# Two whole gate-and-up blocks of each FFN replaced by a tenth seven-product pair

## The chip, the cores and the metric

The kernel runs on one core of a Trainium2 chip. The metric is the device time of one execution in microseconds (us). The engines are TensorE (PE, with its weight load PEld), VectorE (DVE), ScalarE (ACT), GpSimd (POOL) and SyncE (SP, which issues most DMAs). Each engine works off its own list of instructions in order.

## The reference

A trunk of two layers over 512 tokens of width 1024, in float32. Layer 0 has multi-head latent attention, layer 1 chunked attention with a relative bias; each is followed by a SwiGLU feed-forward network (FFN) of width 2816. The change is in the FFN and in the step into it:

```python
x = x + rms_norm(y, attn_post_g[layer])
h = rms_norm(x, ffn_pre_g[layer])
f = swiglu(h, ffn_w_gate[layer], ffn_w_up[layer], ffn_w_down[layer])
x = x + rms_norm(f, ffn_post_g[layer])

def swiglu(h, w_gate, w_up, w_down):
    return (jax.nn.silu(h @ w_gate) * (h @ w_up)) @ w_down
```

## The kernel before

Every float32 operand is split into a high and a low part (`split`: ACT casts `hi`, DVE subtracts to get `lo`, lines 144 and 145), and every product is three matmuls, hi x hi, lo x hi and hi x lo. Tensors are held transposed: 128 features on the partitions, 512 tokens along the row, so x is eight tiles of 128x512.

`ffn` (line 1134), called once per layer, does this:

- `out_proj` makes the attention's output projection in two halves of tokens, h = 0 and 1. `Post` adds up the squares of the result on PE (`tot`), takes the root on POOL, spreads it over the partitions on PE (`bc`), and adds the normed result to x, which `fetch` reads from memory ahead of the projection.
- The FFN's width is 22 blocks of 128. The first two blocks' gate and up (four PSUM banks, `b`) are made by `half(0)` and `half(1)`, 256 tokens each, as soon as that half of x is there. The pre-norm's row factor `rb` is applied only afterwards, to the gate.
- Blocks three and four follow as whole products of 512 columns (`proj`). While PE does these, `blocks_of` prepares four combined inputs `tb` (tiles `th`, `tl`, out of the scaled copies `xg` and the differences `t`), and the norm's `tot` and `bc` are done in between. `gt` is then the gated tile.
- The other 18 blocks are nine pairs in `products` (line 1517): a two-by-two scheme by seven products (j = 0 to 6) instead of eight, of 24 matmuls with 256 columns each, accumulated in the banks `be` (products 0 and 6), `al` (1, 3, 4, 5) and `ga` (2). Copies to `gt` and `ut` on ACT and sums on DVE put the results together.
- `down` then makes the last product of the FFN, also by seven products.

The weights come through `Feed`, a planned list: `load` issues the DMA into a ring of five tiles `raw`, `split` makes `whi` and `wlo` two steps ahead of the product. A `Pair` also needs sums of its four weight quarters: two of them are made by DMAs that POOL issues and that add into a tile already loaded (`begin`; `issue_after` holds them behind the last power on POOL), two by DVE (`sums`). For the first pair all of them are made by DVE. `behind(ins)` writes an instruction behind another on its engine.

The order on each engine is set by the scheduler out of the program order and these constraints.

Of the kernel before, what the change touches and what calls it, by code (L numbers as in the profile page):

```python
# [10 lines left out]
F32 = mybir.dt.float32  # L11
# [8 lines left out]
KT = D // P  # L20
# [7 lines left out]
N_WHOLE = 4  # L28
# [40 lines left out]
def trunk(ctx: ExitStack, tc: tile.TileContext, a, out):  # L69
# [80 lines left out]

    class Pair:
# [4 lines left out]
        def __init__(self, src):  # L156
            self.src, self.raw, self.then, self.made = src, {}, None, False

        def tile(self, n, pool_=wp, tag="raw", bufs=5):
            t = pool_.tile([P, 1024], F32, tag=tag, name=name_("raw"), bufs=bufs)  # L160
            nc.sync.dma_start(t, self.src[n])
            return t

        def begin(self):

            r, self.made = self.raw, True
            r[0] = r[3] = r[6] = self.tile(2, wide[0], "sum", 2)
            r[4] = self.tile(2, wide[0], "sum2", 2)
            for j, n in ((0, 3), (4, 0)):
                with tc.issue_after(last_pow[0].ins):  # L170
                    nc.gpsimd.dma_start(r[j], self.src[n], accum_op=OP.add)  # L171

        def load(self, j):

            if j == 0:
                if not self.made:
                    self.raw[4] = self.tile(2, wide[0], "sum2", 2)
                self.raw[5] = self.tile(3)
            elif j in (1, 2):
                self.raw[j] = self.tile(j - 1)  # L180

        def sums(self, j):
            def plus(t, x, y):
                V.tensor_tensor(t, x, y, op=OP.add)

            r = self.raw
            if j == 0 and not self.made:
                r[0] = r[3] = r[6] = wide[0].tile([P, 1024], F32, tag="sum", name=name_("raw"), bufs=2)
                plus(r[0], r[4], r[5])
            elif j in (3, 6):  # L190
                plus(r[j], r[j], r[j // 3])
            elif j == 4 and not self.made:
                plus(r[4], r[4], r[1])
            elif j == 1 and self.then:
                self.then.begin()
# [68 lines left out]
    class Feed:  # L264


        def __init__(self):
            self.plan, self.raw, self.ready, self.pos, self.room = [], [], [], 0, {}
            self.behind, self.gate, self.low = {}, None, None
# [4 lines left out]
        def add_pairs(self, src):  # L274

            n = src.shape[0]
            pairs = [Pair(src[p]) for p in range(n)]
            for p, pair in enumerate(pairs):
                pair.then = pairs[p + 1] if p + 1 < n else None
                for j in range(7):  # L280
                    self.plan.append((pair, 1024, j, None))
# [7 lines left out]
        def load(self, i):  # L289
            while len(self.raw) <= min(i, len(self.plan) - 1):  # L290
                src, n, j, _ = self.plan[len(self.raw)]
                if isinstance(src, Down):
                    src.load(*j)
                    self.raw.append(None)
                    continue
                if isinstance(src, Pair):
                    src.load(j)
# [314 lines left out]
    class Post:  # L612
# [54 lines left out]
        def apply(self, x, h, each, to=None):  # L667
            c = HALF[h]
            for k in range(KT):
                t = self.y[k][:, c]  # L670
                with first(80 * h):
                    V.tensor_tensor(t, t, self.r[h][:, c], op=OP.mult)
                    if to is None:
                        V.tensor_tensor(x[k][:, c], x[k][:, c], t, op=self.op)
                    else:
                        (nc.gpsimd if k in (0, 2, 4) else V).tensor_tensor(to(k), x[k][:, c], t, op=self.op)
                    each(k, h)

    def fetch(src, make=U):
        x = []  # L680
        for k in range(KT):
            t = make(name="x")
            nc.sync.dma_start(t, src[:, k])
            x.append(t)
        return x

    def out_proj(rhs, n_k, post, have, n_last, late):
# [35 lines left out]
        for h in range(2):  # L723
# [17 lines left out]
            if not h:  # L741
                feed.ahead(2 if late else 3)
# [40 lines left out]
    def plan_ffn(i):  # L783
        for c in range(4):
            feed.add(a["w_gu0"][i, c], 1024, room="h")
        for f in range(N_WHOLE - 2):
            for c in range(2):
                feed.add(a["w_gu"][i, f, c], 1024)
        feed.add_pairs(a["w_pair"][i])
        feed.add_down(a["w_down"][i])  # L790
# [343 lines left out]
    def ffn(i, x_src, osp, firsts, late=()):  # L1134
# [10 lines left out]
        x = fetch(x_src)  # L1145
        post = Post(G_APOST[i], H)
        last = out_proj(osp, KT, post, firsts, 2, late)
# [25 lines left out]
        tb = []  # L1173
        more = blocks_of(x, G_FPRE[i], H, tb)
        next(more)
        b = [bank(), bank()]
        rest = proj(2, KT, 4, xs, b)
        some(rest, 3)
        v = sx.sum.total()
        r = rstd(v)  # L1180
        eps = sp.tile([P, 4], F32, tag="eps", name=f"eps_{i}", bufs=1)
        V.tensor_scalar(eps, v, EPS, None, op0=OP.mult)
        some(rest, 7)
        rb = spread_sb(r)
        next(more)
        banks.extend(b)
        hid = Hidden(H)


        for f in range(N_WHOLE):  # L1190
            if f < 3:
                b = banks[2 * f:2 * f + 2]
                if f == 2:
                    run(rest)
            else:
                b = [bank(), bank()]
                run(proj(2, KT, 4, xs, b))
            t = U(name="gt")
            V.tensor_tensor(t, b[0], rb, op=OP.mult)
            nc.scalar.activation(t, t, AF.Silu)  # L1200
            h = hid.room()
            V.scalar_tensor_tensor(h, t, -1.0, b[1], op0=OP.mult, op1=OP.mult)
            hid.add(h)
            if f == 1:
                next(more)
        products(xs, tb, rb, hid, by_tokens(H) if i else None)
# [108 lines left out]
    def blocks_of(x, gain, make, out):  # L1315
# [3 lines left out]
        for k in range(KT // 2):  # L1319
            out.append([(U(F32R, "th"), U(F32R, "tl")) for _ in range(2)])  # L1320
# [9 lines left out]
        for k in K2:  # L1330
# [3 lines left out]
            split(*cut(out[k][0], A1), m[:, A1])  # L1334
        yield
        for k in K2:
# [3 lines left out]
            split(*out[k][1], n)  # L1340
        yield

    class After:
# [3 lines left out]
        def __init__(self, layer, eps, make):  # L1347
# [4 lines left out]
            self.x, self.later = None, []  # L1352
# [74 lines left out]
        def during(self, j, i):  # L1427
            if j == Down.E3 and i == 1:
                self.x = fetch(a["mid"])
                self.split = Split(self.x, None)  # L1430
# [89 lines left out]
    def products(xs, tb, rb, hid, aside=None):  # L1520
# [5 lines left out]
                  [cut(xs[k + K2], A1) for k in range(K2)]]  # L1526
        pairs = (NF - N_WHOLE) // 2
        for p in range(pairs):
            al, ga = [], []
            be = [bank("t" if p % 2 else "s", "be") for _ in range(2)]  # L1530
            gate = [U(name="gt") for _ in range(2)]
            up_ = [U(name="ut") for _ in range(2)]
            for j in range(7):
                if aside is not None and p and j in (0, 1, 3, 5):
                    next(aside, None)
# [8 lines left out]
                for e in range(2):  # L1544
# [10 lines left out]
                    elif j == 1:  # L1555
                        nc.scalar.copy(t[:, A0], o)
                    elif j == 2:
                        V.tensor_tensor(t[:, A0], t[:, A0], o, op=OP.add)
# [6 lines left out]
                    else:  # L1565
                        V.tensor_tensor(t[:, A1], t[:, A1], o, op=OP.add)
                        V.tensor_tensor(t, t, rb, op=OP.mult)
                        nc.scalar.activation(t, t, AF.Silu)
                        h = hid.room()
                        V.tensor_tensor(h, t, u, op=OP.mult)  # L1570
                        hid.add(h)
# [212 lines left out]
def _layout(i):  # L1784
# [37 lines left out]
    o["w_gu"] = np.stack([np.stack([_chunks(gu[l], fc(f), 4) for f in range(2, N_WHOLE)]) for l in range(2)])  # L1822
# [35 lines left out]
```

## Time and profile before

| what | value |
|---|---|
| median of three runs | 1105.42 us (1103.71 to 1106.43) |
| the profiled execution | 1105.07 us |
| its span in the profile | 1103.3 us |
| mean granted clock of TensorE | 0.997 |
| HBM traffic | 145 GB/s over the span |

A row of the trace gives the start in us, the duration (of all instructions, where "x4" says that several are put together), the engine, the source line, the operation with output<-input, and in brackets how long the engine stood idle before it and for whom. A row of the chain of waits gives the start, the duration, the engine and the number of instructions put together.

### The profile page before, as it was taken

How to read it: one execution, taken by the hardware profiler on the slowest of the kernel's cores; microseconds unless marked ns; L12 is line 12 of the kernel's file. 1: busy time of each engine (PE TensorE's matmuls, PEld its weight loads, DVE VectorE, ACT ScalarE, POOL GpSimd, SP SyncE). 2: the span in 40 equal slices, each digit the busy share in tenths (PEclk: the TensorE clock that was granted, in tenths of full speed). 3: DMA queues.
4: the chain of work that ended last, by engine and by line, in shares of the span. 5: the costliest groups of instructions: out<-in, count | busy, mean ns of one | idle time of the engine just before them, and what ended most of it. 6: DMA issues, size and time to landing. Idle time of an engine off the chain costs nothing.

```text
span 1103.3 us, 19079 instructions
## 1 busy us (share of the span) xinstructions
PE 1092.4 (99%) x6893; PEld 978.8 (89%) x6893; DVE 908.5 (82%) x1659; ACT 678.3 (61%) x1323; POOL 117.1 (11%) x181
## 2 busy tenths in 40 slices
PE   9999999999999999999999999999999999999997
PEld 6887889999999998888888888889899999998885
DVE  7787747988878889978858898758988889789977
ACT  7575737655555556668636767657645555556675
POOL 2211100101000001500000110000100010001401
PEclk9999999999999999999999999999999999999999
DMA  7344226447787757961555677634638888758913
GB/s 240 120 116 142 62 68 238 143 116 184 171 202 184 180 167 248 164 191 49 190 153 156 173 192 186 168 121 161 198 103 214 228 207 223 216 178 249 171 29 76
DMA packets 88334, 181.47 MB, mean 164 GB/s; under 512 B 26816, under 2 KB 28608, under 8 KB 88240
## 3 DMA queue, kind: packets, MB, share of 16 engines
q1 hardware_dynamic: 74752, 147.10, 43.1%
q0 software_dynamic: 13056, 32.73, 16.4%
q8 instruction: 54, 0.88, 0.3%
q10 hardware_dynamic: 432, 0.44, 0.1%
q14 instruction: 40, 0.33, 0.1%
HBM read 148.88 MB, written 10.88 MB: 145 GB/s over the span
## 4 chain that ended last, share of the span: by engine, by line
PE 97%; DVE 1%; ACT 1%; issue 1%; DMA 0%; POOL 0%; DVEq 0%; POOLq 0%; SPq 0%; ACTq 0%
PE al L1550 19%; PE b L377 11%; PE b L378 11%; PE b L379 11%; PE be L1550 9%; PE al L1306 8%; PE be L1306 5%; PE ga L1550 5%; PE de L1306 3%; PE ga L1306 3%; PE pt L561 2%; PE b L1707 2%; PE b L1107 1%; PE sc L1699 1%; PE sc L1698 1%
## 5 line engine op out<-in xcount | busy, mean ns | idle before, releaser
L144 ACT CAST whi<-raw 128x1024 fp32r<-128x1024 f32 (+3 forms) x220 | 221.0, 1006 | 205.6 <-PE al L1550 71.5
L145 DVE TENSOR_TENSOR wlo<-raw,whi 128x1024 fp32r<-128x1024 f32 (+3 forms) x220 | 255.8, 1164 | 67.1 <-ACT whi L144 66.1
L1550 PE MATMUL al<-th,whi 128*128 128x256 f32 x432 | 122.8, 284 | 0.0
L1550 PE MATMUL al<-th,wlo 128*128 128x256 f32 x432 | 121.0, 280 | 0.0
L1550 PE MATMUL al<-tl,whi 128*128 128x256 f32 x432 | 121.0, 280 | 0.0
L377 PE MATMUL b<-xh,whi 128*128 128x512 f32 x234 | 96.7, 415 | 0.0
L378 PE MATMUL b<-xl,whi 128*128 128x512 f32 x234 | 91.8, 392 | 0.0
L379 PE MATMUL b<-xh,wlo 128*128 128x512 f32 x234 | 91.7, 392 | 0.0
L1550 PEld LDWEIGHTS al<-th,whi 128*128 128x128 f32 x432 | 81.3, 188 | 2.2
L1550 PEld LDWEIGHTS al<-th,wlo 128*128 128x128 f32 x432 | 81.3, 188 | 0.2 <-DVE wlo L145 0.2
L1550 PEld LDWEIGHTS al<-tl,whi 128*128 128x128 f32 x432 | 81.3, 188 | 0.0
L548 ACT ACTIVATE p<-p,mn 128x128 f32<-128x128 f32 (+1 forms) x96 | 54.1, 563 | 36.0 <-DVE mn L546 34.1
L145 DVE TENSOR_TENSOR ptl<-pt,pth 128x128 fp32r<-128x128 f32 (+1 forms) x96 | 46.6, 485 | 30.5 <-ACT pth L144 29.6
L145 DVE TENSOR_TENSOR wlo<-wd,whi 128x512 fp32r<-128x512 f32 x86 | 56.3, 684 | 14.6 <-ACT whi L144 14.4
L144 ACT CAST whi<-wd 128x512 fp32r<-128x512 f32 x86 | 49.8, 618 | 25.0 <-PE al L1306 10.7
L144 ACT CAST pth<-pt 128x128 fp32r<-128x128 f32 (+1 forms) x96 | 40.3, 422 | 32.2 <-PE pt L561 31.3
L171 POOL DMA_DIRECT2D raw<-in_w_pair x32 | 28.1, 895 | 285.9 <-DVE ut L1562 84.1
L379 PEld LDWEIGHTS b<-xh,wlo 128*128 128x128 f32 x234 | 43.9, 188 | 9.9 <-DVE wlo L145 0.3
L1306 PE MATMUL al<-whi,pl 128*128 128x512 f32 x132 | 51.5, 390 | 0.0
L1306 PE MATMUL al<-wlo,ph 128*128 128x512 f32 x132 | 51.4, 389 | 0.0
L1306 PE MATMUL al<-whi,ph 128*128 128x512 f32 x132 | 51.4, 389 | 0.0
L377 PEld LDWEIGHTS b<-xh,whi 128*128 128x128 f32 x234 | 44.2, 189 | 5.7 <-ACT whi L144 0.2
(320 smaller groups left out, 3391.2 us busy)
## 6 DMA issues: line engine op xcount, KB each, us to landing
raw<-in_w_pair SPq DMA_DIRECT2D x88, 512.0 KB, 4.6
raw<-in_w_pair POOLq DMA_DIRECT2D x32, 512.0 KB, 7.6
wd<-in_w_down SPq DMA_DIRECT2D x54, 256.0 KB, 6.0
raw<-in_w_o SPq DMA_DIRECT2D x16, 512.0 KB, 4.0
raw<-in_w_gu SPq DMA_DIRECT2D x16, 512.0 KB, 4.7
raw<-in_w_down SPq DMA_DIRECT2D x16, 512.0 KB, 4.3
raw<-in_w_qkb SPq DMA_DIRECT2D x16, 512.0 KB, 3.5
wd<-in_w_down POOLq DMA_DIRECT2D x22, 256.0 KB, 5.0
```

The source lines that it names most:

```text
L144: return (nc.scalar.copy(dst_hi, src), V.tensor_tensor(dst_lo, src, dst_hi.bitcast(F32), op=OP.subtract))
L145: V.tensor_tensor(dst_lo, src, dst_hi.bitcast(F32), op=OP.subtract))
L171: nc.gpsimd.dma_start(r[j], self.src[n], accum_op=OP.add)
L377: nc.tensor.matmul(o, l[0], r[0], start=start, stop=False)
L378: nc.tensor.matmul(o, l[0], r[1], start=False, stop=False)
L379: last_mm[0] = nc.tensor.matmul(o, l[1], r[0], start=False, stop=stop)
L548: nc.scalar.activation(p[:, :n], p[:, :n], AF.Exp, bias=mn[:, :1], scale=-1.0, accum_out=self.sums[:, qt:qt + 1])
L561: nc.tensor.transpose(t[:, kt * P:(kt + 1) * P], p[:, kt * P:(kt + 1) * P], ident)
L1107: nc.tensor.matmul(o[:, q_], va[kt][:, part, v_], pt[:, kt, q_], start=n + kt == 0, stop=n == 2 and kt == NQT - 1)
L1306: nc.tensor.matmul(to[e], l[c], r[d], start=j < 4 and k == 0 and n == 0, stop=k == NF // 2 - 1 and n == 2, skip_group_check=True)
L1550: nc.tensor.matmul(o, l[c], r[d], start=first_ and n == 0, stop=k == K2 - 1 and n == 2, skip_group_check=True)
L1707: nc.tensor.matmul(o[:, q_], vv, pt[:, kt, q_], start=pt is pth and kt == 0, stop=pt is ptl and kt == NQT - 1)
```

## The change

- `N_WHOLE` falls from 4 to 2: blocks three and four become a tenth pair, which runs first, directly behind `half(1)`. The weights `w_gu` are gone.
- The first pair takes its products in the order 1, 2, 0, 3, 6, 4, 5 (`FIRST_TURN`). Its weight sums are all made by accumulating DMAs of POOL's queue: `begin` is called in the h = 0 step of `Post`, and `chain` adds one sum into the next, from SBUF to SBUF.
- `fetch` of x moves into `out_proj`, between its two halves, behind the weights' loads.
- The banks of the first two blocks are copied to SBUF by ACT (`kept`, tiles `fu`), and their gates are done later. The weight of product 3 is split into a room of its own ("u", tiles `wu`).
- The two steps of `blocks_of` and the weight splits are tied to one another by `feed.behind`. The squares of x are summed in the second pair (p = 1). The root is called at its product 6 and `bc` at product 0 of the third pair (p = 2); in the order both `tot` and `bc` come to stand in that product.
- Gates are put in a list `units` and taken from it one by one at j = 1, 3 and 5 of the pairs p = 2 to 6, and at once in p = 7 to 9; in layer 1 the transposes of x (`aside`) are spread over the pairs from p = 4.

```diff
-N_WHOLE = 4
+N_WHOLE = 2
...
+    FIRST_TURN = (1, 2, 0, 3, 6, 4, 5)
...
+        def chain(self):
+
+            self.add(3, self.raw[0])
+            self.add(6, self.raw[3])
...
+            if not h:
+                with behind(feed.loaded):
+                    next(p for p, *_ in feed.plan[feed.pos:] if isinstance(p, Pair)).begin()
...
-                feed.ahead(2 if late else 3)
+                feed.ahead(2 if late else 4)
+                feed.loaded = get_x(feed.loads[feed.pos + (4 if late else 5)])
...
-        sx.squares(0)
-        post.apply(x, 1, sx.each)
+        base = feed.pos
+        pair = feed.plan[base][0]
+        pair.chain()
+        feed.behind[base + 2] = feed.behind[base + 3] = post.apply(x, 1, sx.each)
+        tb, hid = [], Hidden(H)
+        more = blocks_of(x, G_FPRE[i], H, tb)
+        next(more)
+        feed.ahead(3)
         run(half(1))
-        sx.squares(1)
...
+        kept = [H(name="fu") for _ in banks]
+        for t, b in zip(kept[:2], banks[:2]):
+            nc.scalar.copy(t, b)
+        turned = list(next(more))
+        feed.behind[base + 4] = turned
+        with behind(turned[0]):
+            for t, b in zip(kept[2:], banks[2:]):
+                empty = nc.scalar.copy(t, b)
...
+        def step():
+            feed.split(base + 4)
+            with behind(feed.low):
+                turned[:] = next(more)
+            feed.behind[base + 5] = turned
+
+        side = {(0, 2): step, (1, 1): lambda: sx.squares(0), (1, 4): lambda: sx.squares(1), (1, 6): norm, (2, 0): spread_}
+        units = [lambda f=f: gate(*kept[2 * f:2 * f + 2]) for f in range(N_WHOLE)]
...
+            make = U if p > 6 or p == 5 else hid.make
...
+            for j in (range(7) if p else FIRST_TURN):
+                if (p, j) in side:
+                    side[p, j]()
+                if p > 1 and j in (1, 3, 5) and units:
+                    units.pop(0)()
```

PE, layer 0, from the last matmuls ahead of the step in question. Before, the first pair's first product (`be`) follows the end of block four (`b`):

```order
L377 MATMUL b_2790<-xh_2293,whi_2791 128x512
L378 MATMUL b_2790<-xl_2294,whi_2791 128x512
L379 MATMUL b_2790<-xh_2293,wlo_2792 128x512
L1550 MATMUL be_2858<-th_2606,whi_2821 128x256 [waits Activation_49]
L1550 MATMUL be_2858<-tl_2607,whi_2821 128x256
L1550 MATMUL be_2858<-th_2606,wlo_2822 128x256 [waits DVE_49]
```

After, `half(1)` is followed at once by products 1, 2, 0 and 3 of the first pair; this is the end of product 3, the first matmul of product 4 (whi_2776) and the start of product 6 (whi_2700):

```order
L1584 MATMUL al_2671<-tl_2476,wu_2529 128x256
L1584 MATMUL al_2671<-th_2475,wu_2530 128x256
L1584 MATMUL al_2670<-th_2465,whi_2776 128x256 [waits Activation_49]
L1584 MATMUL be_2664<-xh_2291,whi_2700 128x256 [waits Activation_49]
L1584 MATMUL be_2664<-xl_2292,whi_2700 128x256
L1584 MATMUL be_2664<-xh_2291,wlo_2701 128x256 [waits DVE_49]
```

One matmul of product 4 now stands ahead of product 6, and both wait for ACT. ACT, layer 0, where the combined inputs' last casts (`th`, 512 wide) are made. Before, they stand among the weight casts of the first pair, during the whole blocks:

```order
L144 CAST whi_2821<-raw_2819 128x1024 [waits PE_49,Activation_49]
L144 CAST th_2608<-t_590_2625 128x512 [waits DVE_49]
L144 CAST whi_2870<-raw_2656 128x1024 [waits DMAHW0_49,PE_49,Activation_49]
L144 CAST th_2612<-t_594_2633 128x512 [waits DVE_49]
L144 CAST th_2616<-t_598_2641 128x512 [waits DMAHW2_49,DVE_49,Activation_49]
L144 CAST th_2620<-t_602_2649 128x512 [waits DMAHW4_49,DVE_49,Activation_49]
```

After, they stand behind the copies of the kept banks and between the copies of products 1 and 3, which wait for PE:

```order
L1199 COPY fu_2642<-b_2264 128x512 [waits PE_49]
L1591 COPY gt_2666<-al_2670 128x256 [waits PE_49]
L1591 COPY gt_2667<-al_2671 128x256 [waits PE_49]
L144 CAST whi_2700<-raw_2173 128x1024 [waits DMASW5_49]
L144 CAST th_2465<-t_576_2482 128x512 [waits DVE_49]
L144 CAST th_2469<-t_580_2490 128x512 [waits DVE_49]
L1596 COPY gt_2666<-al_2670 128x256 [waits PE_49]
L1596 COPY gt_2667<-al_2671 128x256 [waits PE_49]
L144 CAST th_2473<-t_584_2498 128x512 [waits DVE_49]
L144 CAST th_2477<-t_588_2506 128x512 [waits DVE_49]
L144 CAST whi_2776<-raw_2175 128x1024 [waits DMASW4_49,Activation_49]
L1588 COPY ut_2668<-be_2664 128x256
```

The cast of product 6's weight, which an accumulating DMA fills, now stands ahead of the four `th`, that of product 4 behind them, and the copy of product 0's bank behind that. DVE makes the differences `t` and the parts `tl` between these casts. The first of them are:

```order
L145 TENSOR_TENSOR wlo_2701<-raw_2173,whi_2700 128x1024 [waits DMASW5_49,PE_49,Activation_49]
L1360 TENSOR_TENSOR t_576_2482<-xg_2480,xg_2479 128x256
L1361 SCALAR_TENSOR_TENSOR t_576_2482<-t_575_2481,xg_2480 128x256
L1360 TENSOR_TENSOR t_580_2490<-xg_2488,xg_2487 128x256
L1361 SCALAR_TENSOR_TENSOR t_580_2490<-t_579_2489,xg_2488 128x256
L145 TENSOR_TENSOR tl_2466<-t_576_2482,th_2465 128x512 [waits Activation_49]
L145 TENSOR_TENSOR tl_2470<-t_580_2490,th_2469 128x512 [waits Activation_49]
L1360 TENSOR_TENSOR t_584_2498<-xg_2496,xg_2495 128x256
```

The third `t` comes behind the `tl` of the first two, and each `tl` waits for its `th` on ACT.

The norm's sum and spread on PE (`tot`, `bc`), layer 0. Before, 21 matmuls of 512 columns stood between them; here are the end of `tot`, the last of these and `bc`:

```order
L473 MATMUL tot_2671<-ident,acc_2425 128x128 [waits DVE_49]
L473 MATMUL tot_2671<-ident,acc_2425 128x128
...
L378 MATMUL b_2655<-xl_2276,whi_2658 128x512
L379 MATMUL b_2655<-xh_2275,wlo_2659 128x512
L501 MATMUL bc_2709<-ident,r_2678 128x128 [waits PE_49,Pool_49]
```

After, in product 0 of the third pair:

```order
L484 MATMUL tot_3145<-ident,acc_2938 128x128 [waits DVE_49]
L484 MATMUL tot_3145<-ident,acc_2938 128x128 x3
L1584 MATMUL be_3191<-tl_2464,whi_3115 128x256
L1584 MATMUL be_3191<-th_2463,wlo_3116 128x256
...
L1584 MATMUL be_3191<-tl_2472,whi_3115 128x256
L1584 MATMUL be_3191<-th_2471,wlo_3116 128x256
L1584 MATMUL be_3191<-th_2475,whi_3115 128x256
L512 MATMUL bc_3197<-ident,r_3152 128x128 [waits Pool_49]
```

Nine matmuls of 256 columns stand between them now. In layer 0's output projection the same two, for h = 0, stood 15 matmuls apart and now stand six apart.

More of the change, by code (lines that the diff above doesn't have):

```diff
@@ L186, in sums @@
             r = self.raw
[L187 to L190, printed above, removed]
+            if j in (3, 6) and not self.turn[0]:
                 plus(r[j], r[j], r[j // 3])
-            elif j == 4 and not self.made:
-                plus(r[4], r[4], r[1])
-            elif j == 1 and self.then:
+            if j == (3 if self.turn[0] else 1) and self.then:
                 self.then.begin()
@@ L268, in __init__ @@
             self.plan, self.raw, self.ready, self.pos, self.room = [], [], [], 0, {}
-            self.behind, self.gate, self.low = {}, None, None
+            self.behind, self.gate, self.low, self.loads = {}, None, None, {}
         def add(self, src, n, gain=None, room=None):
@@ L279, in add_pairs @@
                 pair.then = pairs[p + 1] if p + 1 < n else None
-                for j in range(7):
-                    self.plan.append((pair, 1024, j, None))
+                if not p:
+                    pair.turn = FIRST_TURN
+                for j in pair.turn:
+                    self.plan.append((pair, 1024, j, None if p or j != 3 else "u"))
         def add_down(self, src):
@@ L296, in load @@
                 if isinstance(src, Pair):
-                    src.load(j)
+                    self.loads[len(self.raw)] = src.load(j)
                     self.raw.append(None)
@@ L676, in apply, with fetch, out_proj @@
                         (nc.gpsimd if k in (0, 2, 4) else V).tensor_tensor(to(k), x[k][:, c], t, op=self.op)
[L677 to L687, printed above, removed]
+                    at = each(k, h)
+            return at
+    def fetch(src, x, after=None):
+        with behind(after):
+            for k in range(KT):
+                t = U(name="x")
+                ins = nc.sync.dma_start(t, src[:, k])
+                x.append(t)
+        return ins
+    def out_proj(rhs, n_k, post, have, n_last, late, get_x):
         done = list(have)
@@ L785, in plan_ffn @@
             feed.add(a["w_gu0"][i, c], 1024, room="h")
-        for f in range(N_WHOLE - 2):
-            for c in range(2):
-                feed.add(a["w_gu"][i, f, c], 1024)
         feed.add_pairs(a["w_pair"][i])
@@ L1144, in ffn @@
         feed.room["h"] = halves_of(lambda: H(F32R, "wh"))
-        x = fetch(x_src)
+        feed.room["u"] = halves_of(lambda: U(F32R, "wu"))
+        x = []
         post = Post(G_APOST[i], H)
-        last = out_proj(osp, KT, post, firsts, 2, late)
+        last = out_proj(osp, KT, post, firsts, 2, late, lambda after: fetch(x_src, x, after))
         sx = Split(x, G_FPRE[i], H)
@@ L1174, in ffn @@
[L1174 to L1180, printed above, removed]
-        eps = sp.tile([P, 4], F32, tag="eps", name=f"eps_{i}", bufs=1)
[L1182 to L1199, printed above, removed]
+        kept = [H(name="fu") for _ in banks]
@@ new lines, in ffn, with norm @@
+        for t, b in zip(kept[:2], banks[:2]):
[5 more added lines that the diff above has]
+                empty = nc.scalar.copy(t, b)
+        eps = sp.tile([P, 4], F32, tag="eps", name=f"eps_{i}", bufs=1)
+        rb = []
+        def norm():
+            v = sx.sum.total(None, 300)
+            with first(300):
+                r = rstd(v)
+            V.tensor_scalar(eps, v, EPS, None, op0=OP.mult)
+            rb.append(r)
@@ L1200, in ffn, with spread_, gate @@
+        def spread_():
+            rb[0] = spread_sb(rb[0])
+        def gate(t, u):
+            V.tensor_tensor(t, t, rb[0], op=OP.mult)
             nc.scalar.activation(t, t, AF.Silu)
             h = hid.room()
-            V.scalar_tensor_tensor(h, t, -1.0, b[1], op0=OP.mult, op1=OP.mult)
+            V.scalar_tensor_tensor(h, t, -1.0, u, op0=OP.mult, op1=OP.mult)
             hid.add(h)
-            if f == 1:
-                next(more)
-        products(xs, tb, rb, hid, by_tokens(H) if i else None)
+        def step():
[3 more added lines that the diff above has]
+            feed.behind[base + 5] = turned
@@ L1207, in ffn @@
+        side = {(0, 2): step, (1, 1): lambda: sx.squares(0), (1, 4): lambda: sx.squares(1), (1, 6): norm, (2, 0): spread_}
+        units = [lambda f=f: gate(*kept[2 * f:2 * f + 2]) for f in range(N_WHOLE)]
+        products(xs, tb, rb, hid, side, units, empty, turned, by_tokens(H) if i else None)
         post = (AfterLast if i else After)(i, eps, H)
@@ L1319, in blocks_of @@
         for k in range(KT // 2):
-            out.append([(U(F32R, "th"), U(F32R, "tl")) for _ in range(2)])
+            out.append([tuple(m(F32R, n) for n in ("th", "tl")) for m in (U, make if k else U)])
         K2 = range(KT // 2)
@@ L1351, in __init__ @@
             self.v = sp.tile([P, 4], F32, tag="ssv", name=f"ssv_{layer}", bufs=1)
-            self.x, self.later = None, []
+            self.x, self.later = [], []
         GROUPS = ((0,), (1,), (2,), (3,), (4, 5))
@@ L1428, in during @@
             if j == Down.E3 and i == 1:
-                self.x = fetch(a["mid"])
+                fetch(a["mid"], self.x)
                 self.split = Split(self.x, None)
@@ L1518, in plus_x, with products @@
                 queue.dma_start(rows_of(i)[:, o * S:o * S + S][:, c], t[:, c])
-    def products(xs, tb, rb, hid, aside=None):
+    def products(xs, tb, rb, hid, side, units, empty, turned, aside=None):
         K2 = KT // 2
@@ L1526, in products, with gated @@
                   [cut(xs[k + K2], A1) for k in range(K2)]]
+        def gated(t, u):
+            V.tensor_tensor(t, t, rb[0], op=OP.mult)
+            nc.scalar.activation(t, t, AF.Silu)
+            h = hid.room()
+            V.tensor_tensor(h, t, u, op=OP.mult)
+            hid.add(h)
         pairs = (NF - N_WHOLE) // 2
@@ L1530, in products @@
             be = [bank("t" if p % 2 else "s", "be") for _ in range(2)]
[L1531 to L1534, printed above, removed]
+            make = U if p > 6 or p == 5 else hid.make
+            gate = [make(name="gt") for _ in range(2)]
+            up_ = [make(name="ut") for _ in range(2)]
+            for j in (range(7) if p else FIRST_TURN):
[3 more added lines that the diff above has]
+                    units.pop(0)()
+                if aside is not None and p > 3 and j in (0, 2, 4, 6):
                     next(aside, None)
@@ L1555, in products @@
                     elif j == 1:
-                        nc.scalar.copy(t[:, A0], o)
+                        with behind(None if p else empty):
+                            nc.scalar.copy(t[:, A0], o)
                     elif j == 2:
-                        V.tensor_tensor(t[:, A0], t[:, A0], o, op=OP.add)
+                        with behind(None if p else turned[1]):
+                            V.tensor_tensor(t[:, A0], t[:, A0], o, op=OP.add)
                     elif j == 3:
@@ L1566, in products @@
                         V.tensor_tensor(t[:, A1], t[:, A1], o, op=OP.add)
[L1567 to L1571, printed above, removed]
+                        units.append(lambda t=t, u=u: gated(t, u))
+                        while p > 6 and units:
+                            units.pop(0)()
     post = ffn(0, a["x"], osp, firsts)
```

34 lines of the change are left out of this document (19 added, 15 removed).

## The prediction

> **What bounds the kernel now.** I read the page's busy shares and chain first, then windows inside both FFNs, then the list of TensorE's (PE's) waits.
>
> ```profile
> span 1103.3 us, 19079 instructions
> PE 1092.4 (99%) x6893; PEld 978.8 (89%) x6893; DVE 908.5 (82%) x1659; ACT 678.3 (61%) x1323; POOL 117.1 (11%) x181
> PE 97%; DVE 1%; ACT 1%; issue 1%; DMA 0%; POOL 0%; DVEq 0%; POOLq 0%; SPq 0%; ACTq 0%
> ```
> ```profile
> 200.00:300.00 100.00, 100.00 (x756) 95.65 (x756) 87.97 (x151) 58.39 (x100) 8.15 (x9) 1.00 0.61 161
> 300.00:400.00 100.00, 100.00 (x844) 99.37 (x843) 83.48 (x118) 54.63 (x85) 7.03 (x8) 1.00 0.68 173
> ```
> ```profile
> PE sc L1094 <- ACT kh L144: 1.9, 1, 1.9
> ```
>
> PE is 97% of the chain, and in the FFN (a window's columns are its stretch, its length, then the busy time of PE, weight load, DVE, ACT, POOL, and the granted clock) it never idles. So PE work that goes away is time saved, and each wait that PE gets is time added. DVE, at 88 and 83 of 100 us, and ACT, at 58 and 55, have room on the mean; what matters is whether they are on time at one place.
>
> **The PE work saved.** One layer's third and fourth blocks were 96 matmuls of 512 columns. The rows below give the rates: from 220.06 to 234.59 PE goes through 64 matmuls (their places in the order), and the chain of waits has the same stretch of al matmuls of two pairs, eight pairs apart.
>
> ```profile
> 212.07 0.40 PE L377 MATMUL b<-xh,whi 128*128 128x512 f32 x1
> 220.06 0.39 PE L378 MATMUL b<-xl,whi 128*128 128x512 f32 x1
> 234.59 0.39 PE L379 MATMUL b<-xh,wlo 128*128 128x512 f32 x1
> ```
> ```profile
> 243.43 8.65 PE al L1550 x72
> 403.11 8.70 PE al L1550 x72
> ```
>
> 14.53/64 = 0.2270 us a step, so the two blocks took 96 x 0.2270 = 21.79 us. From 243.43 to 403.11 are eight pairs: 159.68/8 = 19.96 us a pair, or 0.1188 us for each of its 168 matmuls. One pair for two blocks saves 21.79 - 19.96 = 1.83 us a layer, **-3.7 us** in all. It lies wholly on the path. The Trainium skill ("TensorE: Matmul & The Clock Gate", Back-to-back issue gap) states N/2.4 ns plus about 2.5 ns for a warm matmul of N columns: an estimate by it is 20.7 us for the blocks and 18.3 for the pair, a saving of 4.8 in all, and a sum 1.1 lower; the trace's steps, 11 and 10 ns longer, disagree with it and decide.
>
> **What stands ahead of the first pair's fifth product.** Let E be the end of the second half's matmuls, where the pair now starts (212.07 before). Its first four products are 96 x 0.1188 = 11.4 us, so PE comes to the matmul al<-th,whi_2776, written ahead of the product be<-xh,whi_2700, at E + 11.4. In-order ACT makes whi_2776 only after the copies of the kept blocks, two weight casts (wu, product 3), four scalings (xg), eight casts of th, four copies of al and whi_2700. Before, this work was spread over the 22 us of the whole blocks. Their durations:
>
> ```profile
> 162.03 0.59 ACT L1112 COPY of<-b 128x512 f32<-128x512 f32 x1 [2.67 <-PE b L1107]
> 162.51 1.15 ACT L144 CAST wh<-raw 128x512 fp32r<-128x512 f32 x2
> 195.20 1.99 ACT L144 CAST whi<-raw 128x1024 fp32r<-128x1024 f32 x2
> 215.93 1.33 ACT L1332 ACTIVATE xg<-x,gains 128x512 f32<-128x512 f32 x2
> 217.17 1.00 ACT L144 CAST th<-t 128x256 fp32r<-128x256 f32 x3
> 230.35 1.66 ACT L144 CAST th<-t 128x512 fp32r<-128x512 f32 x3
> 236.43 0.37 ACT L1554 COPY ut<-be 128x256 f32<-128x256 f32 x1
> 236.69 0.64 ACT L1200 ACTIVATE gt<-gt 128x512 f32<-128x512 f32 x1
> ```
> ```profile
> 194.75 1.22 DVE L145 TENSOR_TENSOR wlo<-raw,whi 128x1024 fp32r<-128x1024 f32 x1
> 214.25 0.75 DVE L1326 TENSOR_TENSOR t<-xg 128x256 f32<-128x256 f32 x2
> 232.74 0.68 DVE L145 TENSOR_TENSOR tl<-t,th 128x512 fp32r<-128x512 f32 x1
> ```
>
> The copy at 162.03 is followed 0.48 us later, so a step frees ACT about 0.1 before its end; the others are taken likewise. The first kept copy can start when its bank is done, nine matmuls before E: E - 1.07. Then come 4 copies x 0.48, 2 weight halves x 0.53, 4 scalings x 0.60, 4 half casts x 0.30 and 2 copies of al x 0.26 (236.43 to 236.69): 7.1 us. So whi_2700 starts at E + 6.1. From there ACT and DVE hand work to and fro, since DVE makes each t only after the tl of the one before: whi 1.04, wlo 1.22, two t 1.40 (a t of 512 is two of 214.25's), two tl 1.2, t 0.70, th 0.62, tl 0.68, t 0.70, th 0.62, whi 0.94: 9.1 us. whi_2776 is there at E + 15.2, hand-off and one copy of be behind it (product 6 writes into that bank again) make E + 15.4: **PE waits 4.0 us, in both layers, +8.0.** Bounds: ACT's two copies of al stand ahead of whi_2776 and wait for the fourth product's end, so even an ACT that is never late needs 0.26 + 2 x 0.52 + 1.04 and two hand-offs behind E + 11.4, a wait of 2.6; with a hand-off of 0.15 us (below) on each of the chain's steps it is 5. I take 4.0, nearer to the rows.
>
> **The clock behind the wait.** The one long wait of PE in the trace:
>
> ```profile
> 104.27 0.48 PE L379 MATMUL b<-ckh,wlo 128*128 128x512 f32 x1
> 106.67 0.50 PE L1094 MATMUL sc<-kh,qh 128*128 128x128 f32 x2 [1.92 <-ACT kh L144]
> ```
> ```profile
> 106.00:108.00 2.00, 1.33 (x7) 1.14 (x7) 2.00 (x4) 1.60 (x4) 0.54 (x1) 0.88 0.76 196
> 108.00:110.00 2.00, 2.00 (x11) 2.00 (x10) 1.38 (x5) 0.49 (x2) 0.52 (x1) 0.50 1.02 408
> 110.00:112.00 2.00, 2.00 (x10) 1.90 (x10) 1.86 (x5) 1.22 (x3) 0.00 (x0) 0.77 0.33 98
> ```
>
> After 1.92 us of idleness the granted clock is 0.88, 0.50 and 0.77 of full in three stretches of 2 us: 2 x (0.12 + 0.50 + 0.23) = 1.7 us of PE time lost. A wait of 4.0 should cost the same: **+3.4** in the two layers (bounds 0 and 6.8, double). The Trainium skill ("TensorE: Matmul & The Clock Gate", The HAM clock gate (the "warmup" mystery)) states half clock after at least one idle window of about 3.4 us that runs free. By an estimate from that rule, a wait of 4.0 holds a whole window in (4.0 - 3.4)/3.4, 18% of the cases, and the term would mostly be zero, the sum 3.4 lower, which is rival B's. The trace's drop after 1.92 speaks against it.
>
> **Sums that PE makes and waits for.** The norm's total and its spread over the partitions (tot, then bc) now stand at the start of the third pair with nine 256-column matmuls between them, where 21 of 512 columns stood; in layer 0's output projection six matmuls stand between instead of 15.
>
> ```profile
> 214.14 0.60 PE L473 MATMUL tot<-ident,acc 128*128 128x128 f32 x4
> 215.48 0.68 DVE L476 TENSOR_REDUCE ss<-tot 128x4 f32<-128x512 f32 x1
> 216.31 1.06 POOL L483 TENSOR_TENSOR r<-ss,mhalf 128x4 f32<-128x4 f32 x1 [22.41 <-DVE ss L476]
> ```
> ```profile
> 180.65 0.38 PE L473 MATMUL tot<-ident,acc 128*128 128x128 f32 x2
> 181.07 0.42 DVE L476 TENSOR_REDUCE ss<-tot 128x2 f32<-128x256 f32 x1 [1.01 <-PE tot L473]
> 181.67 0.71 POOL L483 TENSOR_TENSOR r<-ss,mhalf 128x2 f32<-128x2 f32 x1 [51.70 <-DVE ss L476]
> ```
>
> Reduce to POOL is 0.15 of hand-off (216.16 to 216.31). For four columns the chain behind tot's start is 0.35 of matmuls, some 0.3 to the reduce, 0.68, 0.15 and 1.06: about 2.6 us; PE has 0.35 + 9 x 0.1188 = 1.4 to do: a wait of 1.2 a layer, **+2.4** (0, if POOL's span is overstated, to 3.4). For two columns it is 180.65 to 182.45, 1.8, against 0.24 + 6 x 0.1188 = 0.95: **+0.85**, in layer 0 alone (0 to 1.2).
>
> **Priced at nothing.** The chained sums: after the h=0 pow (now near 184) the first sum is issued, the others behind the h=1 pow.
>
> ```profile
> raw<-in_w_pair POOLq DMA_DIRECT2D x32, 512.0 KB, 7.6
> ```
> ```profile
> 193.10 0.80 POOL L483 TENSOR_TENSOR r<-ss,mhalf 128x2 f32<-128x2 f32 x1 [10.71 <-DVE ss L476]
> ```
>
> Two links of 7.6 from 193.9 on are done at 209.1; whi_2700 needs the second at E + 6.1 = 218.2. Nine us of slack cover it; were a link to take over 12, the excess would be added twice, in both layers. The later fetch of x runs beside the projection, its transfers issued from about 177 and needed from 185. Gates spread over pairs three to eight: a pair then costs DVE seven wlo and two weight sums of that size x 1.14 (1.22 less the overlap), twelve operations of 256 x 0.335 and five of 512 x 0.6: about 17.3 of 19.96 us, 18.2 with layer 1's transposes. DVE covers it, though without more room; if it were 5% slower, PE would wait about 1 us a pair.
>
> **Sum.** -3.7 + 8.0 + 3.4 + 2.4 + 0.85 = +10.95; 1105.07 (the profiled execution, 0.35 below the median of the runs) gives **1116.0**.
>
> **Rivals.** B: the waits come, the clock stays. For it: no wait of this length in the trace, and the gate may look at more than the wait's length. Against: the drop at 106.67. Time: 1116.0 - 3.4 = 1112.6, with waits of 3.3 to 4.6 about 1111 to 1114.
> C, on the other side: ACT reaches whi_2700 at E + 4.5 instead of E + 6.1, that is, with steps a quarter shorter than the rows. From there on the wait is at its floor, 2.6 a layer; if that leaves the clock alone, -3.7 + 5.2 + 0.85 and 0 to 2.4 for the third pair: 1107.4 to 1109.8, in its middle within 0.3% (3.3 us, what a measurement of this kernel can tell from no change). Against: ACT is in order and its first copy can't start ahead of its bank.
> D: PE isn't held at all, because the order is worked off without those waits: 1105.07 - 3.7 = 1101.4. Only durations half as long would allow it.
> E: more than A. The clock falls at the 1.2 us waits too (1.7 each, three of them, 1121), or DVE falls behind in pairs three to eight (1 us each, twelve of them, 1128).
>
> **How the numbers follow.** A, my forecast, 0.52 (1114 to 1118); B 0.26; C 0.11; D 0.03; E 0.08. A, B and the upper half of C are over 80%; the range is 1108 to 1120, from C's middle to A with waits of 5. Faster: D and a remainder, 0.05. Same: C's lower half and a mis-sized saving, 0.10. Slower: 0.85.
>
> **What would show it.** Right: in the first pair of each layer one idle time of PE of about 4 us before al or be, ended by ACT's whi; granted clock under 1 in the 4 us behind it; bc at the start of the third pair waiting for POOL for about 1.2; pairs at 19.96 us from the fourth on. Wrong: no such idle time, or one ended by a DMA (the chained sums late), or idle time of PE ended by DVE's wlo in pairs three to eight. The least certain term is the clock, then the second 1.2.

## The result and the profile after

The changed kernel takes 1145.25 us (median of four, 1144.06 to 1145.96) against 1105.58: a ratio of 1.036, 95% interval 1.0342 to 1.0378. It is slower, as forecast, but by 39.7 us instead of 10.6; the range ended at 1120. The profiled execution took 1145.96.

The page, and the list of PE's waits (what PE waited for, sum in us, times, longest):

```profile
span 1144.2 us, 19424 instructions
PE 1104.4 (97%) x7037; PEld 992.1 (87%) x7037; DVE 918.2 (80%) x1675; ACT 691.2 (60%) x1355; POOL 129.5 (11%) x193
```
```profile
PE al L1584 <- ACT whi L144: 8.6, 2, 4.3
PE al L1328 <- DVE pl L145: 6.1, 2, 3.9
PE al L1328 <- ACT ph L144: 5.6, 4, 1.7
PE bc L512 <- POOL r L494: 4.2, 3, 1.8
```

The first and the last row are the waits of the prediction. The two between stand on line 1328, in `down`, of which the prediction says nothing. To see where the time went, the starts of a few matmuls are enough: the first product of the first pair, the last product of the last pair, and the last matmul of `down`, in both layers. After:

```profile
213.34 0.28 PE L1584 MATMUL al<-xh,whi 128*128 128x256 f32 x1
...
424.53 0.28 PE L1584 MATMUL be<-xh,wlo 128*128 128x256 f32 x1
...
533.05 0.47 PE L1328 MATMUL be<-whi,pl 128*128 128x512 f32 x1
...
797.97 0.28 PE L1584 MATMUL al<-xh,whi 128*128 128x256 f32 x1
...
1007.70 0.29 PE L1584 MATMUL be<-xh,wlo 128*128 128x256 f32 x1
...
1136.59 0.39 PE L1328 MATMUL be<-whi,pl 128*128 128x512 f32 x1
```

Before (layer 0 starts at 212.07, the row shown above; layer 1 at the first matmul of its block three):

```profile
414.37 0.29 PE L1550 MATMUL be<-xh,wlo 128*128 128x256 f32 x1
...
521.56 0.48 PE L1306 MATMUL be<-whi,pl 128*128 128x512 f32 x1
...
787.20 0.40 PE L377 MATMUL b<-xh,whi 128*128 128x512 f32 x1
...
989.68 0.28 PE L1550 MATMUL be<-xh,wlo 128*128 128x256 f32 x1
...
1095.76 0.39 PE L1306 MATMUL be<-whi,pl 128*128 128x512 f32 x1
```

| stretch | before | after | difference |
|---|---|---|---|
| up to layer 0's E | 212.07 | 213.34 | +1.3 |
| layer 0, E to the last product | 202.30 | 211.19 | +8.9 |
| layer 0, `down` | 107.19 | 108.52 | +1.3 |
| up to layer 1's E | 265.64 | 264.92 | -0.7 |
| layer 1, E to the last product | 202.48 | 209.73 | +7.3 |
| layer 1, `down` | 106.08 | 128.89 | **+22.8** |

The sum is 40.8. Some 17 us are in the parts that the prediction worked out. 24 are in `down`, nearly all of it in layer 1's, which the change does not touch in the code.

**The first pair.** Rows of PE, of ACT ahead of them, and windows around the wait of layer 0 (the number behind the engines' columns is the granted clock):

```profile
229.35 0.58 PE L1584 MATMUL al<-th,whi 128*128 128x256 f32 x1 [4.28 <-ACT whi L144]
...
813.98 0.58 PE L1584 MATMUL al<-th,whi 128*128 128x256 f32 x1 [4.28 <-ACT whi L144]
```
```profile
227.73 0.62 ACT L144 CAST th<-t 128x512 fp32r<-128x512 f32 x1 [1.43 <-DVE t L1361]
228.26 1.04 ACT L144 CAST whi<-raw 128x1024 fp32r<-128x1024 f32 x1
```
```profile
228.00:230.00 2.00, 0.65 (x2) 0.65 (x3) 1.62 (x4) 2.00 (x5) 0.86 (x1) 0.62 0.37 29
230.00:232.00 2.00, 2.00 (x11) 2.00 (x11) 2.00 (x2) 0.79 (x1) 0.00 (x0) 0.50 0.78 133
232.00:234.00 2.00, 2.00 (x11) 2.00 (x11) 0.46 (x2) 0.00 (x0) 0.00 (x0) 0.50 1.05 313
234.00:236.00 2.00, 2.00 (x14) 2.00 (x13) 0.42 (x1) 1.02 (x1) 0.03 (x1) 0.68 0.77 313
```

PE waits 4.28 us for the cast of product 4's weight, which stands behind the last `th`, which waits for DVE's `t`: the chain that was worked out, with 4.0. Behind it the clock is at half from about 228.5 to 235.3 (1.5 us of the first window, all of the next two, 1.3 of the last), 6.8 us where 3.4 followed the 1.92 us wait before. Some 0.85 us of it lie ahead of 229.35, where PE still waits and loses nothing by them.

**The third pair.** bc waits longer than the estimate of 1.2:

```profile
264.50 0.65 PE L512 MATMUL bc<-ident,r 128*128 128x128 f32 x4 [1.76 <-POOL r L494]
```

**Layer 1's last pairs and `down`.** Two neighbouring rows of the tile `hd` (a gate times up, one for each of the 22 blocks) on DVE, then SP's queue from the end of the products on:

```profile
934.34 0.68 DVE L1553 TENSOR_TENSOR hd<-gt,ut 128x512 f32<-128x512 f32 x1
...
1004.44 0.68 DVE L1553 TENSOR_TENSOR hd<-gt,ut 128x512 f32<-128x512 f32 x1
```
```profile
1008.01 1.97 SPq L1247 DMA_DIRECT2D out_x<-xt  x4
...
1018.43 5.35 SPq L1247 DMA_DIRECT2D out_x<-xt  x8
1023.83 0.50 SPq L1241 DMA_DIRECT2D x<-mid  x1
1024.37 0.91 SPq L241 DMA_DIRECT2D wd<-in_w_down  x2
...
1029.81 19.02 SPq L241 DMA_DIRECT2D wd<-in_w_down  x25
```

The same of before:

```profile
939.94 2.15 SPq L1225 DMA_DIRECT2D out_x<-xt  x4
...
979.68 0.33 SPq L232 DMA_DIRECT2D wd<-in_w_down  x1
```

For 70 us no hd is made; eight of the 22 come in a heap when the products end. In layer 0 it is the same (none between 349.68 and 412.16). In layer 1 five of the eight transposes of x fall into the heap as well, and SP issues the writes of their results (`out_x`) and the loads for the next ones in turn with the weights of `down`: the first `wd` is issued 16.7 us after the last product, where it was 10.0 us ahead of it before. What PE then does, in windows of 10 us:

```profile
1010.00:1020.00 10.00, 4.43 (x19) 3.07 (x18) 10.00 (x21) 3.75 (x6) 0.00 (x0) 0.85 0.32 75
1020.00:1030.00 10.00, 6.79 (x17) 4.71 (x18) 6.46 (x13) 1.23 (x3) 0.00 (x0) 0.67 0.74 181
1030.00:1040.00 10.00, 8.49 (x20) 5.74 (x19) 3.95 (x7) 1.96 (x4) 1.64 (x2) 0.50 0.87 283
1040.00:1050.00 10.00, 8.74 (x36) 6.48 (x35) 7.13 (x11) 6.35 (x11) 1.12 (x3) 0.96 1.07 344
```

In these 40 us PE idles for 11.5, and the clock that is missing is worth another 10 (part of it while PE idles). DVE is full in the first window only, so it is not DVE alone.

My theory, ahead of the experiments: the large pool of an FFN has 40 places, which was the number of results to keep (20 of the 22 hd, 20 sums). The change puts six parts of the combined inputs, which live until the last product, into that pool (and, for a shorter time, the kept banks and the gates and ups of most pairs), so that hd and x's tiles wait for places; the heap and the late transposes follow from this, and the late weights from SP's order.

### The profile page after: what moved, and what is told of

Same layout as the page of the kernel before. It is cut to its first block, busy times and chain, and to the rows that moved or that the text cites. A ratio compares the mean times of both kernels' runs of the same rounds, so it can differ in the third digit from the quotient of the medians.

```text
span 1144.2 us, 19424 instructions
## 1 busy us (share of the span) xinstructions
PE 1104.4 (97%) x7037; PEld 992.1 (87%) x7037; DVE 918.2 (80%) x1675; ACT 691.2 (60%) x1355; POOL 129.5 (11%) x193
## 5 line engine op out<-in xcount | busy, mean ns | idle before, releaser
L1584 PE MATMUL al<-th,whi 128*128 128x256 f32 x464 | 132.5, 285 | 9.0 <-ACT whi L144 8.6
L1584 PE MATMUL al<-tl,whi 128*128 128x256 f32 x464 | 130.1, 280 | 0.0
L1584 PE MATMUL al<-th,wlo 128*128 128x256 f32 x464 | 130.0, 280 | 0.0
L1584 PEld LDWEIGHTS al<-th,whi 128*128 128x128 f32 x464 | 87.6, 189 | 12.0 <-ACT whi L144 9.0
L388 PE MATMUL b<-xh,whi 128*128 128x512 f32 x170 | 71.7, 422 | 0.0
L181 POOL DMA_DIRECT2D raw<-in_w_pair x40 | 35.6, 904 | 287.1 <-DMA raw<-in_w_pair 137.5
L390 PE MATMUL b<-xh,wlo 128*128 128x512 f32 x170 | 66.8, 393 | 0.0
L389 PE MATMUL b<-xl,whi 128*128 128x512 f32 x170 | 66.8, 393 | 0.0
L1584 PE MATMUL be<-xh,whi 128*128 128x256 f32 x160 | 46.9, 294 | 0.0
L1584 PE MATMUL be<-xl,whi 128*128 128x256 f32 x160 | 46.8, 293 | 0.0
```

What stands on the lines that cost most here:

```text
L181: nc.gpsimd.dma_start(self.raw[j], src, accum_op=OP.add)
L388: nc.tensor.matmul(o, l[0], r[0], start=start, stop=False)
L389: nc.tensor.matmul(o, l[0], r[1], start=False, stop=False)
L390: last_mm[0] = nc.tensor.matmul(o, l[1], r[0], start=False, stop=stop)
L1584: nc.tensor.matmul(o, l[c], r[d], start=first_ and n == 0, stop=k == K2 - 1 and n == 2, skip_group_check=True)
```

## The experiments

**The room (e1_room).** The six long-lived tiles go back to the small pool, six tiles of x, which nothing reads after the second pair, into the large one:

```diff
-                t = U(name="x")
+                t = (make if k > 1 else U)(name="x")
...
-            out.append([tuple(m(F32R, n) for n in ("th", "tl")) for m in (U, make if k else U)])
+            out.append([tuple(m(F32R, n) for n in ("th", "tl")) for m in (U, U)])
```

> Same work, but the combined inputs' six long-lived tiles go back to the small pool and six short-lived tiles of x go to the large one. If the changed kernel's gate results (hd) stop for 60 to 70 us in each layer because the large pool's 40 places are taken, they now come pair by pair, layer 1's down falls from 128.9 us back to about 107 (-22), layer 0's by 1 to 2, and since the copies of product 0's bank also move ahead of the last th, the first pair's wait falls from 4.3 to about 1.5 a layer, with the clock's drop gone: about 1108 (1104 to 1114). Rival: DVE has too much to do in the last pairs whatever the room (the transposes are no earlier by plan): down of layer 1 stays over 120 us and the time over 1125.

Measured: 1113.02 us, a ratio to the kernel before of 1.0072 (1.0057 to 1.0087). The last product and the end of `down` in layer 1:

```profile
997.60 0.28 PE L1584 MATMUL be<-xh,wlo 128*128 128x256 f32 x1
...
1103.64 0.39 PE L1328 MATMUL be<-whi,pl 128*128 128x512 f32 x1
```
```profile
991.91 0.45 SPq L241 DMA_DIRECT2D wd<-in_w_down  x1
```

`down` takes 106.04 us, as before the change, hd comes pair by pair, and SP issues the first `wd` 5.7 us ahead of the last product. DVE has 915.0 us of work, 918.2 in the changed kernel, so the rival (too much to do) falls. In each layer the first pair now waits 0.78 and 0.86, with no drop of the clock: with these rooms ACT makes the copies of product 0's bank ahead of the last `th`. Of the 5 us over my middle value 1.7 are two new waits of 0.72 and 1.01 in the output projections; that x's tiles now take places there which other tiles want is my reading, not tested.

**The transposes early (e2_early).**

```diff
-                if aside is not None and p > 3 and j in (0, 2, 4, 6):
+                if aside is not None and p > 0 and j in (0, 1, 3, 5):
```

> Only the transposes of x are called from the second pair on, as in the kernel before. The gate results still pile up (the order shows it). If the transposes and the writes of their results, between a full pool and the weight loads on SP's queue, are what makes the pile costly in layer 1, its down comes near layer 0's (about 109 us instead of 128.9): about 1126 (1122 to 1130). Rival: the pile of gate results on DVE alone is the cost: down stays at 120 or more, time over 1137.

Measured: 1124.87 us (1.0181, 1.0166 to 1.0196), as the first theory said.

```profile
1008.09 0.28 PE L1584 MATMUL be<-xh,wlo 128*128 128x256 f32 x1
...
1116.80 0.39 PE L1328 MATMUL be<-whi,pl 128*128 128x512 f32 x1
```

The heap of hd is still there (none between 932.65 and 996.41), but `down` takes 108.7 us. So the heap alone costs some 2.6 us in layer 1; layer 0, where it stands alone in the changed kernel too, lost 1.3.

**The other queue (e3_queue).** The loads of x and the writes of the transposed tiles by POOL:

```diff
-            nc.sync.dma_start(x, a["mid"][:, k])
+            nc.gpsimd.dma_start(x, a["mid"][:, k])
...
-                nc.sync.dma_start(
+                nc.gpsimd.dma_start(
```

> Only the loads of x for the transposes and the writes of their results go to POOL's queue; pile and late transposes stay. If down's weights are late because SP's queue stands behind these writes, the waits after the first two of layer 1's down go and with them most of the half-clock time: -12 to -17, about 1130 (1127 to 1135). Rival: DVE's pile is the cost: -3 at most, over 1140.

Measured: 1173.05 us (1.0614, 1.0598 to 1.063), 28 us more than the changed kernel where the theory had 12 to 17 less and the rival at most 3 less (its "over 1140" holds in the number alone): PE waits 7.75 us in layer 1's sixth pair and 12.1, 6.3 and 6.8 in `down`. POOL's queue also carries the sums of weights, so this run seems to move the jam into another queue; it does not tell what SP's order costs.

**The transposes late, without the heap (e5_late).** On e1_room:

```diff
-                if aside is not None and p > 3 and j in (0, 2, 4, 6):
+                if aside is not None and p > 6:
...
+        for _ in aside or ():
+            pass
```

> The version e1_room (1113.0) with the transposes of x called only in the last three pairs, and what is left of them behind the last pair. Gate results come pair by pair, so only the lateness of the transposes and of their writes on SP's queue is left of the cost in layer 1. If late writes alone hold up the weights of down, layer 1's down goes from 106 to 112 or more: 1119 to 1128. Rival: it takes the pile of gate results as well, which makes DVE late and SP wait for it: 1113 to 1115.

Measured: 1128.83 us (1.0232, 1.0216 to 1.0248), just above the first theory's range.

```profile
996.73 0.28 PE L1584 MATMUL be<-xh,wlo 128*128 128x256 f32 x1
...
1118.88 0.39 PE L1328 MATMUL be<-whi,pl 128*128 128x512 f32 x1
```
```profile
1010.86 0.71 DVE L1244 STREAM_TRANSPOSE xt<-x 128x512 f32<-128x512 f32 x1 [1.13 <-DMA x<-mid]
```
```profile
1008.16 0.86 SPq L241 DMA_DIRECT2D wd<-in_w_down  x2
...
1011.60 1.97 SPq L1247 DMA_DIRECT2D out_x<-xt  x4
1013.61 18.30 SPq L241 DMA_DIRECT2D wd<-in_w_down  x25
```

hd comes pair by pair, yet `down` takes 122.2 us: 16 more than in e1_room. The first two weight loads are issued 11.4 us behind the last product; the last transpose is at 1010.86, SP's write follows at 1011.60, and right behind it come the other 25. With e1_room, e2_early and the changed kernel, that is a square: neither late 106.0, only hd 108.7, only the transposes 122.2, both 128.9. The transposes' lateness is the larger part. Both together cost some 4 us more than the two alone; the square is not quite clean, since with the heap the last transpose is later as well, at 1027.04, 19 us behind the last product instead of 14.

**The same with the other queue (e7_late_pool).** e5_late and the edit of e3_queue:

> The version e5_late (1128.8: gate results on time, transposes only in the last three pairs), with the loads of x for the transposes and the writes of their results on POOL's queue instead of SP's. If the weights of down are late because SP issues them in order behind these writes, they are now issued on time and layer 1's down falls from 122 to 106 to 110 us: 1113 to 1117. Rival: the late transposes cost through DVE, or the transfers themselves are in the way of the weights: it stays at 1124 or more. A third way: POOL's own sums of down's weights stand behind the writes now: 1118 to 1128, with waits for these sums.

Measured: 1156.61 us (1.047, 1.0453 to 1.0488), a miss, in the direction of the third way but beyond it. SP's row, PE's longest wait, and the longest of SP's waits between 1000 and 1060:

```profile
1011.45 0.86 SPq L241 DMA_DIRECT2D wd<-in_w_down  x2
```
```profile
PE de L1328 <- DVE wlo L145: 10.5, 1, 10.5
```
```profile
SPq L241 <- DMA out_x<-xt: 26.5, 4, 13.1
```

POOL issues the writes one by one, with 1.9 to 5.1 us of idleness between those of a tile, the last transpose slips to 1048.87, and DVE, in order, waits 12.85 us for its x. The last row shows a second tie beside SP's order: with the writes on another queue, the loads of `wd` still wait for them, 26.5 us in all. Part of `wd` comes from the large pool, like x's tiles, so this is most likely their places. It stays open how much of the 16 us of e5_late is SP's order, and how much are the places or the transposes' waiting on DVE. That the weights of `down` are issued late together with the transposes is shown; the share of each is not.

**The first pair (e4_step).** On the changed kernel:

```diff
-        side = {(0, 2): step, ...
+        side = {(0, 3): step, ...
```

> Only the step that makes the 512-wide combined inputs is called one product later, which puts ACT's copies of product 0 ahead of the four 512-wide casts, and product 6 ahead of all of product 4 on PE. By the chain of the prediction product 4's weight is still there at E + 15.2, but PE needs it at E + 14.3: a wait of about 1.0 in place of 4.28 in both layers (-6.6), and if a wait that short leaves the clock alone another -6.8: about 1132 (1130 to 1135). Rival: the clock falls at a wait of 1 us as well: about 1138.5; or the wait moves to another place whole: 1145.

Measured: 1137.62 us (1.0295, 1.0278 to 1.0312). The wait of 4.28 is now 1.47, with 0.52 behind it, in both layers. Windows from 230 on (layer 0) and 811 on (layer 1), the clock behind the engines:

```profile
230.00:232.00 2.00, 2.00 (x10) 2.00 (x11) 2.00 (x2) 0.50 (x1) 0.00 (x0) 0.54 0.88 215
232.00:234.00 2.00, 2.00 (x13) 2.00 (x12) 0.56 (x2) 0.00 (x1) 0.00 (x0) 0.60 0.88 268
...
811.00:813.00 2.00, 1.48 (x12) 1.39 (x12) 2.00 (x3) 1.20 (x2) 0.00 (x0) 1.00 0.81 141
```

In layer 0 the clock fell for (0.46 + 0.40) x 2 / 0.5 = 3.4 us, in layer 1, at the same waits, not at all. The gain of 7.6 us lies between the two theories, nearer to the rival's 6.6: the rest of the chain stayed, with 2.0 where 1.0 was expected.

**All of it (e6_fu_dve).** e1_room, bc one product later, and two of the kept banks' copies on DVE:

```diff
-        with behind(turned[0]):
+        with behind(turned[1]):
             for t, b in zip(kept[2:], banks[2:]):
-                empty = nc.scalar.copy(t, b)
+                V.tensor_copy(t, b)
+        empty = turned[0]
...
-(2, 0): spread_}
+(2, 1): spread_}
```

> The version e1_room (1113.0) with two more edits: bc is called one product later (24 matmuls between tot and bc instead of 9), and the last two copies of the kept banks go from ACT to DVE. If the 1.75 us waits at bc are the chain's 3.1 us less the work between, they vanish (-3.5); if the first pair's 0.78 and 0.86 come from ACT's 7.1 us of work ahead of product 6's weight, one us less of it takes most of them (-2.5 of 3.3): 1107 (1105.5 to 1109), about level with the kernel before. What is left then of the -3.7 is taken by the waits ahead of the second half (0.7 twice, 1.0). Rival: DVE, now with the two copies, makes the t later, the first pair waits as long or longer: 1109.5 or more.

Measured: 1107.82 us against 1104.36 of the kernel before on the same chip: 1.0034 (1.0022 to 1.0047).

```profile
PE bc L512 <- POOL r L494: 1.7, 2, 1.0
PE be L1585 <- DVE fu L1199: 1.2, 2, 0.6
```

The waits of the third pair are gone; what is left of bc's stands in the output projections. In each layer the first pair waits 0.57 and 0.22. From E to the last product it takes 202.28 us in layer 0 (214.09 to 416.37), and 202.30 did before: what the first two pairs lose at and right behind such small waits, some 1.5, and a few tenths elsewhere take the whole 1.83 that a pair saves. No version beat the kernel before.

## Why the prediction was wrong

- **The saving: right.** Pairs four to nine have periods of 19.9 to 20.2 us, as taken.
- **The wait of the first pair: right.** 4.28 in both layers for 4.0, at the place and for the reason given; e4_step, and e1_room by other rooms, show that the order of that step makes it.
- **The clock: right in kind, mis-sized.** The first pair's period is 27.35 us; less 19.96 and 4.28, 3.1 is lost (2.9 in layer 1), for 1.7. The prediction took one drop behind one wait as the rule, and that it came out on the right side was in part luck: behind the same 4.28 the clock was at half for 3.4 us only in layer 1 of e2_early and of e3_queue, and in e5_late the old wait, 1.93 there, left it at full. The Trainium skill ("TensorE: Matmul & The Clock Gate", The HAM clock gate) has a free-running window of about 3.4 us; the half-speed stretches, 3.4 in e4_step and 6.8 here, agree with one and two of these. Its rule that a whole idle window must pass does not hold here: the clock fell behind the 1.92 before the change and in layer 0 of e4_step, at waits of 1.47 and 0.52, though never behind the 1.76 at bc. That two waits in one window add up is a guess.
- **bc: mis-sized.** 1.76 for 1.2 twice, and 0.71 for 0.85 in layer 0.
- **Failed: the step "Gates spread over pairs three to eight", priced at nothing.** It counted DVE's time, and nothing speaks against that count: PE has no wait for DVE's wlo in those pairs. It did not count the places, and that cost 24 us in `down`, 22.8 of them in layer 1. Which pool a tile comes from (`make` for gate, up and the combined inputs) is in the diff, and the order of the changed kernel shows it too: eight `hd` of each layer stand behind the weight splits of the last pair, where they stood seven splits apart before. I read the order at three places and not there. It also let the transposes go from the second pair to the fifth as if they were only DVE's time, without asking what is queued behind their writes on SP. Rival E had DVE falling behind, with the wrong cause and 0.08.

With the terms as measured, -3.7 + 8.6 + 6.0 + 3.5 + 0.7 = 15.1, the forecast would have been 1120. Of the 26 us that are left, 24 are `down`; e1_room, which changes the places alone, gives back `down`'s 22.8 in layer 1. Some 1.6 us, most of them at the end of layer 0's last pair, where the heap begins, were not followed further.

## What to carry to other kernels

A tile's pool is a resource with a queue, like an engine: for every tile that a change lets live longer, count the places at the moment when most are taken, and look in the order for results that come in a heap. When work that is off the critical path is put later, price what stands behind its transfers on their queue, not only its own time. A saving of 1.8 us in 20 is gone with four waits of half a microsecond, so the step into a new first pair must be as well fed as the middle ones.

## What the runs showed of the hardware

The granted clock fell to half for 3.4 us or a whole multiple of it: in windows of 1 us, every stretch ahead of the last matmul is 3.4, 6.8, 10.2, 13.7 or 17.1 us long, in all nine traces. What sets one off is less regular. A wait of 4.28 us was followed by 6.8 us at half in four cases (both layers here, layer 0 of e2_early and of e3_queue) and by 3.4 in two; a wait of 1.92 by 3.4 in eight traces and by none in e5_late:

```profile
106.00:108.00 2.00, 0.85 (x4) 0.70 (x5) 2.00 (x3) 2.00 (x5) 0.08 (x1) 1.00 0.66 144
```

No single wait of 1.76 or less brought one; two in close succession did now and then: 1.47 and 0.52 in one layer of e4_step and not in the other, 1.28 and 0.22 in e7_late_pool (at 1089) and not in the changed kernel (1.28 and 0.18). A short stall thus cost up to about its own length again, and sometimes nothing. In e7_late_pool POOL took 0.66 us to issue a write of a transposed tile, and the next of the same tile started 2.5 to 5.8 us after it, while SP issued four in about 2 us.
